# Strassen products of a SwiGLU block in another order: adding on one another in PSUM, with a growing weight sum

## The chip, the cores and the metric

The kernel runs on one core of a Trainium2 chip. The metric is the time of one execution on the device in microseconds (us). A profiled execution gives the trace that the text reads: TensorE (PE, its weight loads PEld), VectorE (DVE), ScalarE (ACT), GpSimd (POOL), SyncE (SP, which here issues the DMAs), and the DMA queues.

## The reference

One decoder layer in fp32 on 512 tokens of width 2048: an RMS norm, an input projection, three token mixers, an output projection onto the residual, and a SwiGLU feed-forward part of inner width 5632.

```python
x = x + mix @ w_out[l]
h2 = _rms_norm(x, norm2_g[l])
x = x + (jax.nn.silu(h2 @ w_gate[l]) * (h2 @ w_up[l])) @ w_down[l]
```

The change touches the last of these lines alone.

## The kernel before

Each fp32 product is made of three matmuls: every operand is split into a high part (fp32r) and a low rest, and high x high, high x low and low x high are added in PSUM.

Gate, up and down go by a scheme of Strassen's kind: a product of 2 x 2 blocks is made from seven block products instead of eight, on sums of blocks of the activations (`ops`, `acts`) and of the weights. The seven are numbered 1 to 7 after the quarter that they feed; `ORDER`, line 67, is their order in a round. The results (i, k) are collected in SBUF tiles of 128 x 512, two (a = 0 and 1) to each.

- **Up** (class `Up`, from L1288): 22 rounds, u0 to u21, two for each of 11 blocks of gate and up columns, one per half of the inner dimension. The first round of a block starts the tiles (`keep`, L1312), the second adds (`add`) or subtracts (`less`). i = 1 is gate, i = 0 is up. After the second round `gate` (silu on ACT), `weigh` (a multiplication on POOL, L1386) and `turn` make the activations of down.
- **Down** (class `Down`, from L1491): 12 rounds, d0 to d11, of four or three pairs of inner blocks (`RANGES`), into tiles `y`.

A product is two units, A and B. A unit of up is 12 matmuls of 512 columns (L1304, L1306, L1307; down's are L1569 to L1571) with one weight block of 128 x 1024, in two PSUM banks. Products alternate between two pairs of banks (`outs`). A matmul with start=True begins a bank afresh; before, that is so in products 7, 1, 5 and 2, so that 4 adds to 7, 6 to 1, and 3 to 5. After each product `done` reads the two banks into the tiles; what is read is the sum so far. Product 6 (with 1 below it) is wanted in three results, so `six` (L1332 in Up, L1586 in Down) reads each of its banks three times on DVE, or in down twice on DVE and once by an ACT copy (`copy_u`, L1594) that POOL then subtracts (L1579).

**Weights.** A block arrives by DMA from SP (`pump`, L243) in one of the raw buffers named "21a", "21b", "22a", "22b", "11", "12", "sa", "sb"; a block's names 11, 12, 21, 22 are its quarters of the weight. `plus` (L169; the instruction is L172) adds two raw blocks on POOL, 128 x 1024. `split_up_to` (from L264) makes the three tiles that PE needs: wn, a copy of the high part in PSUM (ACT, L283), wh, the same in SBUF (ACT, L284), and wl, the rest (DVE, L285, the raw block minus wn). `next_unit` (L307) calls it two units ahead (`SPLIT_AHEAD`), and there are three buffers of wh and wl each. `last` says whether a split is the last reader of its raw block and gives up its buffer.

A round's 14 units have the numbers base to base + 13, A and B by turns. Their seven blocks are, before: s, 11, 22, 11, 21, 12, 11, where four sums on POOL change what stands in them: s = 21 + 11 (written out at unit base - 4 and base - 3), 21 += 22 (base, base + 1), 11 = 21 + 11 (base + 2, + 3) and 11 += 12 (base + 7, + 8). `sums` holds them by the unit at which they are written out, and each engine executes its own instructions in the order written. The dictionary `bufs` says which raw buffer holds which block, and is turned around after each round, so that a round loads while the one before computes.

**Around u0** the input of gate and up is still being prepared. DVE makes the sums of blocks of h (L1128 to L1136), the low rests of them (L1148), and the sum of squares for the norm (L97), each with both inputs in SBUF; xr is the residual (L1098).

**The last rounds** turn finished tiles by DVE transposes (`turn_back`, L1478) into tiles z that lie in raw buffers no longer used (`BACK`), and SP writes them out (`put`, L1488). The last product, 3 of d11, is cut in three pieces; its last one is transposed on PE (`sides`, L1534), copied (L1537) and written (L1556). `later(n, f, ...)` puts a call off by n units in a queue of evictions or of extras.

Of the kernel before, what the change touches and what calls it, by code (L numbers as in the profile page):

```python
# [13 lines left out]
AF = mybir.ActivationFunctionType  # L14
ALU = mybir.AluOpType
# [50 lines left out]

ORDER = (7, 1, 4, 6, 5, 2, 3)
TH = T // 2
# [48 lines left out]
def kernel(ctx: ExitStack, tc: tile.TileContext, xT, wi, wo, wgu, wd, cst_in, outT):  # L117
# [57 lines left out]
    def up_block(pair, m, half, j):  # L175
# [3 lines left out]

    bufs = {"A": dict(zip(("21", "11", "s", "22"), ("21a", "22a", "sa", "22b"))),  # L180
            "B": dict(zip(("21", "11", "s", "22"), ("21b", "11", "12", "sb")))}

    for n in range(2 * NBLOCKS):
        base = len(works)
        keys = {c: {k: (k, f"u{n}{c}") for k in ("11", "12", "21", "22", "s")} for c in "AB"}
        for k in ("21", "11", "22", "12"):
            for i, c in enumerate("AB"):
                entries.append((bufs[c]["s" if k == "12" else k], keys[c][k],
                                up_block(n // 2 * 2, 2 - int(k[0]), int(k[1]) - 1, n % 2 * 4 + 2 * i)))
        for i, c in enumerate("AB"):  # L190
# [8 lines left out]
        bufs = {c: {"21": b["22"], "11": b["21"], "s": b["s"], "22": b["11"]} for c, b in bufs.items()}  # L199

# [5 lines left out]
    for t, (g, r) in enumerate(DOWN):  # L206
        first, end = RANGES[r]
        base = len(works)
        keys, size = {}, {}
        for c, (lo, hi) in {"A": (first, first + 2), "B": (first + 2, end)}.items():  # L210
            keys[c] = {k: (k, f"d{t}{c}") for k in ("11", "12", "21", "22", "s")}
            size[c] = 4 * P * (hi - lo)
            bufs[c]["12"] = bufs[c]["s"]
        for k in ("21A", "11A", "21B", "11B", "22A", "22B", "12A", "12B"):
# [4 lines left out]
        def add(c, out, one, other, buf=None):  # L219
            return plus(keys[c][out], keys[c][one], keys[c][other], size[c], buf)  # L220

        for i, c in enumerate("AB"):
            sums[base - 4 + i].append(add(c, "s", "21", "11", bufs[c]["s"]))
            sums[base + i].append(add(c, "21", "21", "22"))
            sums[base + 2 + i].append(add(c, "11", "21", "11"))
            sums[base + 7 + i].append(add(c, "11", "11", "12"))
        works.extend((keys[c][k], last, "moves") for k, last in (
            ("s", True), ("11", False), ("22", True), ("11", False), ("21", True), ("12", True), ("11", True)) for c in "AB")
        final_bufs = bufs
        bufs = {c: {"21": b["22"], "11": b["21"], "s": b["s"], "22": b["11"]} for c, b in bufs.items()}  # L230

# [1056 lines left out]
    class Up:  # L1288
# [4 lines left out]
        def product(self, q):  # L1293
            banks = outs[:2]
            outs[:] = outs[2:] + banks
            for c in range(2):
                sums_now()
                run(evacs)
                wh, wl = next_unit()
                for a, b in enumerate(banks):  # L1300
                    high, low = slice(a * P, (a + 1) * P), slice(TH + a * P, TH + (a + 1) * P)
                    for f in range(2):
                        x, s = ops[q, self.first + 2 * c + f], slice(f * T, (f + 1) * T)
                        nc.tensor.matmul(b, x[:, high], wh[:, s], start=c == f == 0 and q in (7, 1, 5, 2), stop=False,  # L1304
                                         skip_group_check=True)
                        nc.tensor.matmul(b, x[:, high], wl[:, s], start=False, stop=False, skip_group_check=True)  # L1306
                        nc.tensor.matmul(b, x[:, low], wh[:, s], start=False, stop=c == f == 1, skip_group_check=True)  # L1307
                yield
                run(extras)
            later(0, self.done, self.first == 0, q, banks)  # L1310

        def keep(self, i, k, a, b):  # L1312
            t = self.c[i, k, a] = slot(f"b{self.n}c{i}{k}{a}")
            if a == 0:
                nc.scalar.activation(t, b, AF.Copy, scale=1.0 if i or not self.n else self.scale(k, a))
            elif i or not self.n:
                nc.vector.tensor_copy(t, b)
            else:
                nc.vector.tensor_scalar(t, b, self.scale(k, a), None, op0=ALU.mult)
# [11 lines left out]

        def six(self, by, a, b):  # L1332
            by(0, 1, a, b)
            self.less(0, a, b)
            self.less(1, a, b)

        def done(self, first, q, banks):
            if first and q == 7:
                self.c = {}
            by = self.keep if first else self.add  # L1340
            for a, b in enumerate(banks):
                if q == 7:
                    by(1, 1, a, b)
                elif q == 1:
                    by(0, 0, a, b)
                elif q == 4:
                    by(1, 0, a, b)
                elif q == 6:
                    if a:
                        later(0, self.six, by, a, b)  # L1350
                    else:
                        self.six(by, a, b)
# [6 lines left out]
            if q in (6, 5):  # L1359
                later(1, self.gate, 6 - q, queue=extras)  # L1360
            elif q == 2:
                self.dram = tc.dram_tile([T, T], F32, name=f"bd{self.n}")
# [37 lines left out]
    y = {}  # L1400
# [46 lines left out]
    for n in range(NBLOCKS):  # L1447
        blk = Up(n)
        for blk.first in (0, 4):
# [18 lines left out]
    BACK = {(1, 0, 0): ("22", "A"), (1, 1, 1): ("22", "B"), (1, 1, 0): ("21", "A"), (1, 0, 1): ("21", "B"),  # L1468
            (0, 1, 0): ("s", "A"), (0, 1, 1): ("s", "B"), (0, 0, 0): ("22", "A"), (0, 0, 1): ("22", "B")}

# [20 lines left out]
    class Down:  # L1491
# [9 lines left out]
        def product(self, k, q):  # L1501
            banks = outs[:2]
            outs[:] = outs[2:] + banks
            fresh = q in (7, 1, 5, 2)
            tail = self.end and k == 6
# [70 lines left out]

        def add(self, i, k, a, src, eng=nc.vector, op="tensor_add"):
            t = y[self.sum(i, k, a)]
            getattr(eng, op)(t, t, src)  # L1579

        def less(self, i, k, a, src, eng=nc.vector):
            self.add(i, k, a, src, eng, "tensor_sub")

        def six(self, a, b):
            self.less(1, 1, a, b)
            self.add(0, 1, a, b)  # L1586
            if self.end:
                self.less(1, 0, a, b)
            else:
                later(0, self.copy_u, a, b, queue=extras)  # L1590

        def copy_u(self, a, b):
            u = slot(f"d{self.t}u{a}")
            nc.scalar.copy(u, b)  # L1594
            later(0, self.less, 1, 0, a, u, nc.gpsimd)

        def done(self, q, banks):
            for a, b in enumerate(banks):
                if q == 7:
                    self.add(1, 1, a, b)  # L1600
                elif q == 1:
                    self.add(0, 0, a, b)
                elif q == 4:
                    self.add(1, 0, a, b)
                elif q == 6:
                    if a:
                        later(0, self.six, a, b)
                    else:
                        self.six(a, b)
                elif q == 5:  # L1610
# [108 lines left out]
```

## Time and profile before

| | us |
|---|---|
| three runs | 1843.78, 1844.95, 1843.36 |
| their median | 1843.78 |
| span of the profiled execution | 1840.0 |
| of this, up (576.4 to 1414.3) | 837.9 |
| of this, down (1414.3 to the last matmul, 1834.5) | 420.2 |
| PE busy | 1832.2 |
| DVE, ACT, POOL busy | 1430.0, 1313.4, 1019.0 |

In the rows of the trace's timelines the first number is the start, the second the duration, both in us; then come engine, line and operation, out<-in by the program's names (buffer numbers left out), the shapes, and in brackets how long the engine was idle before and what released it. DMA issues and waits are not counted as busy. A matmul's printed duration is longer than its share of PE, since matmuls are pipelined: the distance of starts is what counts.

### The profile page before, as it was taken

The page shows a single profiled execution, that of the slowest core. Times are in us where ns is not written, and L with a number is a line of the kernel's source. Part 1 is how long each engine was busy: PE and PEld are TensorE (multiplying, and loading weights), DVE is VectorE, ACT ScalarE, POOL GpSimd, SP SyncE. Part 2 cuts the span into 40 slices and gives each one's busy share as a digit, 9 for nine tenths or more (in the row PEclk, how much of TensorE's full clock was granted, in tenths as well). Part 3 has the DMA queues.
Part 4 walks back from the last instruction along what each step waited for, and adds up shares of the span by engine and source line. Part 5 has one row for each costly group of instructions (what it writes and reads, how often), then busy time and mean ns, then how long its engine had stood idle before and what let it go on. Part 6 is the DMA issues. An engine that isn't in the chain of part 4 may idle for free.

```text
span 1840.0 us, 26561 instructions
## 1 busy us (share of the span) xinstructions
PE 1832.2 (100%) x8314; PEld 1521.0 (83%) x8314; DVE 1430.0 (78%) x2023; ACT 1313.4 (71%) x1784; POOL 1019.0 (55%) x793
## 2 busy tenths in 40 slices
PE   9999999999999999999999999999999999999998
PEld 7888888888888888888888888888888888888887
DVE  6689888986689877777777777777777777777777
ACT  6355644553468788887888888888887778877775
POOL 0126543110003557886887767787776558776552
PEclk9999999999999999999999999999999999999999
DMA  7353255363343466777867778677687579877635
GB/s 276 88 150 121 88 145 156 107 178 132 118 138 104 115 160 183 203 205 183 227 179 210 209 185 224 174 207 210 178 273 255 200 232 294 252 259 259 237 121 109
DMA packets 401612, 337.81 MB, mean 184 GB/s; under 512 B 185408, under 2 KB 327872, under 8 KB 401472
## 3 DMA queue, kind: packets, MB, share of 16 engines
q1 hardware_dynamic: 400896, 335.33, 62.9%
q8 instruction: 66, 1.08, 0.2%
q10 hardware_dynamic: 576, 0.79, 0.1%
q14 instruction: 74, 0.61, 0.1%
HBM read 261.61 MB, written 66.03 MB: 178 GB/s over the span
## 4 chain that ended last, share of the span: by engine, by line
PE 73%; DVE 1%; DMA 0%; issue 0%; ACT 0%; DVEq 0%; SPq 0%
PE out L1307 15%; PE out L1304 15%; PE out L1306 15%; PE out L1570 7%; PE out L1569 7%; PE out L1571 7%; PE o L322 2%; PE o L324 2%; PE o L323 2%; DVE y L1579 0%; DVE wl L285 0%; DMA out_T<-z 0%; DVE z L1478 0%; DVE lnv L412 0%; DVE y L1548 0%
## 5 line engine op out<-in xcount | busy, mean ns | idle before, releaser
L1304 PE MATMUL out<-wh,h 128*128 128x512 f32 x1232 | 479.2, 389 | 0.0
L1306 PE MATMUL out<-wl,h 128*128 128x512 f32 x1232 | 479.2, 389 | 0.0
L1307 PE MATMUL out<-wh,h 128*128 128x512 f32 x1232 | 479.2, 389 | 0.0
L1306 PEld LDWEIGHTS out<-wl,h 128*128 128x128 f32 x1232 | 231.2, 188 | 48.1
L1307 PEld LDWEIGHTS out<-wh,h 128*128 128x128 f32 x1232 | 231.2, 188 | 48.1
L1304 PEld LDWEIGHTS out<-wh,h 128*128 128x128 f32 x1232 | 231.2, 188 | 47.9
L1570 PE MATMUL out<-wl,a 128*128 128x512 f32 x620 | 240.4, 388 | 0.1
L1569 PE MATMUL out<-wh,a 128*128 128x512 f32 x620 | 240.4, 388 | 0.0
L1571 PE MATMUL out<-wh,a 128*128 128x512 f32 x620 | 240.3, 388 | 0.0
L289 ACT CAST wh<-w 128x1024 fp32r<-128x1024 f32 (+2 forms) x94 | 97.0, 1031 | 134.3 <-PE o L323 46.0
L1579 DVE TENSOR_TENSOR y<-y,out 128x512 f32<-128x512 f32 x192 | 128.4, 684 | 46.8 <-PE out L1571 45.0
L263 DVE TENSOR_TENSOR wl<-w,wh 128x1024 fp32r<-128x1024 f32 (+2 forms) x95 | 114.4, 1204 | 34.0 <-ACT wh L289 33.8
L1570 PEld LDWEIGHTS out<-wl,a 128*128 128x128 f32 x620 | 116.4, 188 | 24.2 <-DVE wl L285 0.5
L1569 PEld LDWEIGHTS out<-wh,a 128*128 128x128 f32 x620 | 116.4, 188 | 24.1
L1571 PEld LDWEIGHTS out<-wh,a 128*128 128x128 f32 x620 | 116.4, 188 | 23.8
L573 DVE SCALAR_TENSOR_TENSOR y<-bu,cst,y 128x511 f32<-128x511 f32 (+14 forms) x120 | 88.9, 741 | 1.1
L322 PE MATMUL o<-mh_c,wh 128*128 128x512 f32 x128 | 51.0, 398 | 0.0
L322 PE MATMUL cq<-hh,wh 128*128 128x512 f32 x128 | 50.3, 393 | 0.0
L324 PE MATMUL o<-mh_c,wl 128*128 128x512 f32 x128 | 50.0, 391 | 0.0
L323 PE MATMUL o<-ml_c,wh 128*128 128x512 f32 x128 | 50.0, 390 | 0.0
L323 PE MATMUL cq<-hl,wh 128*128 128x512 f32 x128 | 49.9, 390 | 0.0
L324 PE MATMUL cq<-hh,wl 128*128 128x512 f32 x128 | 49.9, 390 | 0.0
(2353 smaller groups left out, 4745.0 us busy)
## 6 DMA issues: line engine op xcount, KB each, us to landing
od<-a SPq DMA_DIRECT2D x154, 256.0 KB
a<-od SPq DMA_DIRECT2D x154, 256.0 KB
w<-in_wi SPq DMA_DIRECT2D x58, 512.0 KB
w<-in_wo SPq DMA_DIRECT2D x32, 512.0 KB
x<-in_xT SPq DMA_DIRECT2D x16, 256.0 KB
xr<-in_xT SPq DMA_DIRECT2D x16, 256.0 KB
x2d<-xr SPq DMA_DIRECT2D x16, 256.0 KB
z<-x2d SPq DMA_DIRECT2D x64, 64.0 KB
```

What stands on the lines that cost most here:

```text
L263: fn(*args)
L289: (nc.vector.tensor_copy if u == 0 else nc.scalar.copy)(hi[:, :n], t[:, :n])
L322: nc.tensor.matmul(out, wh, xh, start=start, stop=False)
L323: nc.tensor.matmul(out, wh, xl, start=False, stop=False)
L324: nc.tensor.matmul(out, wl, xh, start=False, stop=stop)
L1304: nc.tensor.matmul(b, x[:, high], wh[:, s], start=c == f == 0 and q in (7, 1, 5, 2), stop=False, skip_group_check=True)
L1306: nc.tensor.matmul(b, x[:, high], wl[:, s], start=False, stop=False, skip_group_check=True)
L1307: nc.tensor.matmul(b, x[:, low], wh[:, s], start=False, stop=c == f == 1, skip_group_check=True)
L1569: nc.tensor.matmul(b[:, lo:hi], x[:, high], wh[:, s], start=start, stop=False, skip_group_check=True)
L1570: nc.tensor.matmul(b[:, lo:hi], x[:, high], wl[:, s], start=False, stop=False, skip_group_check=True)
L1571: nc.tensor.matmul(b[:, lo:hi], x[:, low], wh[:, s], start=False, stop=last, skip_group_check=True)
L1579: getattr(eng, op)(t, t, src)
```

## The change

The products come in the order 1, 7, 6, 4, 5, 2, 3, and three of them begin a bank: 1, 7 and 2. On the pair of banks of 1, products 6, 5 and 3 are added; on that of 7, product 4; product 2 stands alone on the other pair. So the sum in PSUM after each product is just what one result wants, and every bank is read once for each product. `six`, `copy_u` and the POOL subtraction are gone. The tile (1, 0) of a first round begins as the negative of a bank, by a scale of -1 in `keep`.

The weight blocks are 11, s, s, 22, 21, 12, s. s = 21 + 11 is now followed by s += 22 and, at the end, s += 12 in the same buffer, and 21 += 22 in between. A round's 11 is done with after its first product; 12 comes into its buffer. The units at which the sums are written out move too.

In the last rounds the transposes and puts of the first two results take other places in the queues, and the tiles z of (0, 1) lie where 11 lay.

```diff
-ORDER = (7, 1, 4, 6, 5, 2, 3)
+ORDER = (1, 7, 6, 4, 5, 2, 3)
+FRESH = (1, 7, 2)
...
-    bufs = {"A": dict(zip(("21", "11", "s", "22"), ("21a", "22a", "sa", "22b"))),
-            "B": dict(zip(("21", "11", "s", "22"), ("21b", "11", "12", "sb")))}
+    bufs = {"A": dict(zip(("11", "21", "s", "22"), ("21b", "21a", "22a", "22b"))),
+            "B": dict(zip(("11", "21", "s", "22"), ("11", "sa", "12", "sb")))}
+
+    def use(base, size, keys, c, early):
+        i, key, buf = "AB".index(c), keys[c], bufs[c]["s"]
+        sums[base - early + i].append(plus(key["s"], key["21"], key["11"], size[c], buf))
+        sums[base + 1 + i].append(plus(key["s"], key["s"], key["22"], size[c]))
+        sums[base + 3 + i].append(plus(key["21"], key["21"], key["22"], size[c]))
+        sums[base + 7 + i].append(plus(key["s"], key["s"], key["12"], size[c]))
+
+    BLOCKS = (("11", True), ("s", False), ("s", False), ("22", True), ("21", True), ("12", True), ("s", True))
+
+    def turn_bufs():
+        return {c: {"11": b["22"], "21": b["21"], "22": b["11"], "s": b["s"]} for c, b in bufs.items()}
...
-        for i, c in enumerate("AB"):
-            key = keys[c]
-            sums[base - 4 + i].append(plus(key["s"], key["21"], key["11"], 1024, bufs[c]["s"]))
-            sums[base + i].append(plus(key["21"], key["21"], key["22"], 1024))
-            sums[base + 2 + i].append(plus(key["11"], key["21"], key["11"], 1024))
-            sums[base + 7 + i].append(plus(key["11"], key["11"], key["12"], 1024))
-        works.extend((keys[c][k], last, "moves") for k, last in (
-            ("s", True), ("11", False), ("22", True), ("11", False), ("21", True), ("12", True), ("11", True)) for c in "AB")
+        for c in "AB":
+            use(base, {"A": 1024, "B": 1024}, keys, c, 2 if n else 5)
+        works.extend((keys[c][k], last, "moves") for k, last in BLOCKS for c in "AB")
...
-    def keep(self, i, k, a, b):
+    def keep(self, i, k, a, b, sign=1.0):
...
-    def six(self, by, a, b):
-        by(0, 1, a, b)
-        self.less(0, a, b)
-        self.less(1, a, b)
...
+                if q == 1:
+                    by(0, 0, a, b)
+                elif q == 7:
                     by(1, 1, a, b)
...
+                elif q == 6:
+                    if first:
+                        self.keep(1, 0, a, b, -1.0)
+                    else:
+                        self.less(0, a, b)
                 elif q == 4:
...
+                    self.add(1, 0, a, b)
                 elif q == 5:
                     self.less(1, a, b)
+                elif q == 2:
+                    self.add(0, 0, a, b)
                 else:
-                    self.add(0, q - 2, a, b)
+                    by(0, 1, a, b)
...
-        def copy_u(self, a, b):
-            u = slot(f"d{self.t}u{a}")
-            nc.scalar.copy(u, b)
-            later(0, self.less, 1, 0, a, u, nc.gpsimd)
...
-            if self.end and q == 6:
+            if self.end and q == 4:
...
-                        later((2, 3, 6, 7)[n] + a, turn_back, self.sum(i, k, a))
-                    later((4, 5, 8, 9)[n], put, self.g, i, k, queue=extras)
+                        later((4, 5, 6, 7)[n] + a, turn_back, self.sum(i, k, a))
+                    later((6, 7, 8, 9)[n], put, self.g, i, k, queue=extras)
```

Lines of the changed kernel are two further on here (L172 is L173, L285 is L287, L1148 is L1150, L1317 is L1319; further down L1478 is L1477, L1548 is L1547, and the add and the subtraction of y are L1578 and L1582).

POOL in u0, before; w('21', 'u0A') is the raw block 21 of round u0, unit A:

```order
L172 TENSOR_TENSOR w('s', 'u0A')_5765<-w('21', 'u0A')_5556,w('11', 'u0A')_5609 128x1024
L172 TENSOR_TENSOR w('s', 'u0B')_5814<-w('21', 'u0B')_5559,w('11', 'u0B')_5664 128x1024
L172 TENSOR_TENSOR w('21', 'u0A')_5556<-w('21', 'u0A')_5556,w('22', 'u0A')_5817 128x1024
L172 TENSOR_TENSOR w('21', 'u0B')_5559<-w('21', 'u0B')_5559,w('22', 'u0B')_5872 128x1024
L172 TENSOR_TENSOR w('11', 'u0A')_5609<-w('21', 'u0A')_5556,w('11', 'u0A')_5609 128x1024
L172 TENSOR_TENSOR w('11', 'u0B')_5664<-w('21', 'u0B')_5559,w('11', 'u0B')_5664 128x1024
L172 TENSOR_TENSOR w('11', 'u0A')_5609<-w('11', 'u0A')_5609,w('12', 'u0A')_5881 128x1024
L172 TENSOR_TENSOR w('11', 'u0B')_5664<-w('11', 'u0B')_5664,w('12', 'u0B')_5933 128x1024
```

and in the changed kernel:

```order
L173 TENSOR_TENSOR w('s', 'u0A')_5710<-w('21', 'u0A')_5559,w('11', 'u0A')_5504 128x1024
L173 TENSOR_TENSOR w('s', 'u0B')_5767<-w('21', 'u0B')_5713,w('11', 'u0B')_5661 128x1024
L173 TENSOR_TENSOR w('s', 'u0A')_5710<-w('s', 'u0A')_5710,w('22', 'u0A')_5817 128x1024
L173 TENSOR_TENSOR w('s', 'u0B')_5767<-w('s', 'u0B')_5767,w('22', 'u0B')_5881 128x1024
L173 TENSOR_TENSOR w('21', 'u0A')_5559<-w('21', 'u0A')_5559,w('22', 'u0A')_5817 128x1024
L173 TENSOR_TENSOR w('21', 'u0B')_5713<-w('21', 'u0B')_5713,w('22', 'u0B')_5881 128x1024
L173 TENSOR_TENSOR w('s', 'u0A')_5710<-w('s', 'u0A')_5710,w('12', 'u0A')_5878 128x1024
L173 TENSOR_TENSOR w('s', 'u0B')_5767<-w('s', 'u0B')_5767,w('12', 'u0B')_5933 128x1024
```

The sums into 21 moved from the second place to the third. The second pair now reads and writes s, which the splits of units 2 and 3 read before; the third pair waits for no split; the last pair writes s, which the splits of units 4 and 5 read, where before it wrote 11, which those of units 6 and 7 read.

DVE in u0, before, from the end of the preparation's eight short operations to the weights of units 6 and 7:

```order
L1134 TENSOR_TENSOR ta_5950<-h_7_5924,h_15_6076 128x256
L1135 TENSOR_TENSOR tb_6128<-ta_5950,h_7_5924 128x256
L1136 TENSOR_TENSOR tb_6128<-tb_6128,h_15_6076 128x256
L1317 COPY b0c_6136<-out_5993 128x512
L285 TENSOR_TENSOR wl_6142<-w('11', 'u0A')_5609,wn_6143 128x1024
L285 TENSOR_TENSOR wl_6160<-w('11', 'u0B')_5664,wn_6161 128x1024
```

and in the changed kernel, with the weights of units 4 and 5 ahead of them:

```order
L287 TENSOR_TENSOR wl_6083<-w('s', 'u0A')_5710,wn_6084 128x1024
L287 TENSOR_TENSOR wl_6102<-w('s', 'u0B')_5767,wn_6103 128x1024
L1150 TENSOR_TENSOR h_6_6063<-ta_5901,h_6_6063 128x256
L1150 TENSOR_TENSOR h_6_6065<-tb_5977,h_6_6065 128x256
L1150 TENSOR_TENSOR h_6_6067<-h_14_5973,h_6_6067 128x256
L1150 TENSOR_TENSOR h_6_6069<-tb_5977,h_6_6069 128x256
L1150 TENSOR_TENSOR h_6_6071<-h_14_5973,h_6_6071 128x256
L1136 TENSOR_TENSOR ta_5950<-h_7_5924,h_15_6075 128x256
L1137 TENSOR_TENSOR tb_6124<-ta_5950,h_7_5924 128x256
L1138 TENSOR_TENSOR tb_6124<-tb_6124,h_15_6075 128x256
L1319 TENSOR_SCALAR b0c_6133<-out_5993 128x512
L287 TENSOR_TENSOR wl_6136<-w('22', 'u0A')_5817,wn_6137 128x1024
```

DVE's instructions stand where they stood, with other weights: units 6 and 7 now take 22, which is no sum, and units 4 and 5 take s where they took 22.

DVE in d11, around the reads of the fourth product (6 before, 4 now), before:

```order
L1579 TENSOR_TENSOR y<-y,out_5990 128x512 x3
L285 TENSOR_TENSOR wl_17767<-w('12', 'd11A')_17552,wn_17768 128x1024
L1478 STREAM_TRANSPOSE z_17761<-y 128x16x32
L1579 TENSOR_TENSOR y<-y,out_5991 128x512 x3
L1478 STREAM_TRANSPOSE z_17792<-y 128x16x32
L285 TENSOR_TENSOR wl_17795<-w('12', 'd11B')_17572,wn_17796 128x1024
L285 TENSOR_TENSOR wl_17817<-w('11', 'd11A')_17414,wn_17818 128x1024
L1478 STREAM_TRANSPOSE z_17792<-y 128x16x32
```

and in the changed kernel:

```order
L1578 TENSOR_TENSOR y<-y,out_5990 128x512
L1578 TENSOR_TENSOR y<-y,out_5991 128x512
L287 TENSOR_TENSOR wl_17590<-w('12', 'd11A')_17374,wn_17591 128x1024
L1477 STREAM_TRANSPOSE z_17585<-y 128x16x32
L1477 STREAM_TRANSPOSE z_17612<-y 128x16x32
L287 TENSOR_TENSOR wl_17615<-w('12', 'd11B')_17396,wn_17616 128x1024
L287 TENSOR_TENSOR wl_17637<-w('s', 'd11A')_17364,wn_17638 128x1024
L1477 STREAM_TRANSPOSE z_17612<-y 128x16x32
```

Ahead of the weights of 12 stand two reads of PSUM where six stood, four fewer; the transposes and weights behind them keep their order.

More of the change, by code (lines that the diff above doesn't have):

```diff
@@ L217 @@
             entries.append((bufs[c][k[:2]], keys[c][k[:2]], [down_block(g, int(k[0]) - 1, int(k[1]) - 1, *span)]))
[L219 to L228, printed above, removed]
+        for c in "AB":
+            use(base, size, keys, c, 2)
+        works.extend((keys[c][k], last, "moves") for k, last in BLOCKS for c in "AB")
         final_bufs = bufs
-        bufs = {c: {"21": b["22"], "11": b["21"], "s": b["s"], "22": b["11"]} for c, b in bufs.items()}
+        bufs = turn_bufs()
     splits = {}
@@ L1303, in product @@
                         x, s = ops[q, self.first + 2 * c + f], slice(f * T, (f + 1) * T)
-                        nc.tensor.matmul(b, x[:, high], wh[:, s], start=c == f == 0 and q in (7, 1, 5, 2), stop=False,
+                        nc.tensor.matmul(b, x[:, high], wh[:, s], start=c == f == 0 and q in FRESH, stop=False,
                                          skip_group_check=True)
@@ L1330, in less @@
             nc.vector.tensor_sub(t, t, b)
-        def six(self, by, a, b):
-            by(0, 1, a, b)
-            self.less(0, a, b)
-            self.less(1, a, b)
         def done(self, first, q, banks):
-            if first and q == 7:
+            if first and q == 1:
                 self.c = {}
@@ L1575, in sum, with add, less @@
             return self.g, i, k, a
-        def add(self, i, k, a, src, eng=nc.vector, op="tensor_add"):
+        def add(self, i, k, a, src):
             t = y[self.sum(i, k, a)]
[L1579 to L1590, printed above, removed]
-        def copy_u(self, a, b):
-            u = slot(f"d{self.t}u{a}")
-            nc.scalar.copy(u, b)
-            later(0, self.less, 1, 0, a, u, nc.gpsimd)
+            nc.vector.tensor_add(t, t, src)
+        def less(self, i, k, a, src):
+            t = y[self.sum(i, k, a)]
+            nc.vector.tensor_sub(t, t, src)
         def done(self, q, banks):
             for a, b in enumerate(banks):
-                if q == 7:
+                if q == 1:
+                    self.add(0, 0, a, b)
+                elif q == 7:
                     self.add(1, 1, a, b)
-                elif q == 1:
-                    self.add(0, 0, a, b)
+                elif q == 6:
+                    self.less(1, 0, a, b)
                 elif q == 4:
                     self.add(1, 0, a, b)
[L1605 to L1609, printed above, removed]
                 elif q == 5:
```

34 lines of the change are left out of this document (13 added, 21 removed).

## The prediction

> **What bounds the kernel now.** First I read the page's busy shares and the windows by stage (busy time and number of instructions of PE, PEld, DVE, ACT, POOL, then granted clock).
>
> ```profile
> PE 1832.2 (100%) x8314; PEld 1521.0 (83%) x8314; DVE 1430.0 (78%) x2023; ACT 1313.4 (71%) x1784; POOL 1019.0 (55%) x793
> ```
>
> ```profile
> 576.40:1414.30 837.90, 837.90 (x3699) 693.79 (x3698) 643.90 (x741) 696.33 (x844) 614.16 (x420) 1.00 0.71 195
> 1827.60:1840.00 12.40, 7.00 (x42) 5.51 (x40) 6.78 (x13) 0.70 (x3) 0.00 (x0) 0.91 0.78 153
> ```
>
> TensorE works through all of the up stage, at full clock. The stage has 22 rounds of 14 units: 837.90 / 308 = 2.72 us a unit, 0.227 for each of its 12 matmuls, 38.09 a round. The change keeps every matmul, so work saved on other engines shortens nothing there. Time can only be lost, where a unit's weights come late, or won behind 1827.6, where PE waits. The view of PE's waits has one in that stretch:
>
> ```profile
> PE sides L1534 <- DVE y L1548: 0.6, 1, 0.6
> ```
>
> So I ask of each unit whether its wl, the last step of its weights, is there in time. The least slack is where rounds begin: u0 still shares DVE with the preparation of the input. PE's timeline gives u0's start and the first matmul of unit 6 that reads wl; then DVE's and POOL's timelines of before.
>
> ```profile
> 576.52 0.39 PE L1304 MATMUL out<-wh,h 128*128 128x512 f32 x1
> 593.07 0.39 PE L1306 MATMUL out<-wl,h 128*128 128x512 f32 x1
> ```
>
> ```profile
> 580.62 2.14 DVE L97 TENSOR_TENSOR ssum<-ssum,sr 128x512 f32<-128x512 f32 x1
> ...
> 587.11 0.42 DVE L1148 TENSOR_TENSOR h<-ta,h 128x256 fp32r<-128x256 f32 x1
> 587.44 0.42 DVE L1148 TENSOR_TENSOR h<-tb,h 128x256 fp32r<-128x256 f32 x1
> 587.78 0.42 DVE L1148 TENSOR_TENSOR h<-h,h 128x256 fp32r<-128x256 f32 x1
> 588.11 0.42 DVE L1148 TENSOR_TENSOR h<-tb,h 128x256 fp32r<-128x256 f32 x1
> ...
> 590.03 0.68 DVE L1317 COPY b0c<-out 128x512 f32<-128x512 f32 x1
> 590.64 1.21 DVE L285 TENSOR_TENSOR wl<-w('11', 'u0A')_5609,wn 128x1024 fp32r<-128x1024 f32 x1
> ```
>
> ```profile
> 579.80 2.42 POOL L172 TENSOR_TENSOR w('11', 'u0A')_5609<-w('21', 'u0A')_5556,w('11', 'u0A')_5609 128x1024 f32<-128x1024 f32 x1 [7.78 <-DVE wl L285]
> 582.17 2.87 POOL L172 TENSOR_TENSOR w('11', 'u0B')_5664<-w('21', 'u0B')_5559,w('11', 'u0B')_5664 128x1024 f32<-128x1024 f32 x1
> 591.98 2.42 POOL L172 TENSOR_TENSOR w('11', 'u0A')_5609<-w('11', 'u0A')_5609,w('12', 'u0A')_5881 128x1024 f32<-128x1024 f32 x1 [6.94 <-ACT wh L284]
> ```
>
> Unit 6's wl ends at 590.64 + 1.21 = 591.85, 1.2 us ahead of 593.07. From 585.04 to 591.98 POOL did nothing, and just there DVE ran eight short operations with both inputs in SBUF (five of L1148, L1134 to L1136).
>
> **Two engines, one turn at a time.** Such operations and POOL's sums do not run together. DVE's and POOL's timelines around the first sum:
>
> ```profile
> 547.22 0.42 DVE L1148 TENSOR_TENSOR h<-ta,h 128x256 fp32r<-128x256 f32 x1
> 547.55 2.62 DVE L1148 TENSOR_TENSOR h<-h,h 128x256 fp32r<-128x256 f32 x1
> ```
>
> ```profile
> 547.43 2.46 POOL L172 TENSOR_TENSOR w('s', 'u0A')_5765<-w('21', 'u0A')_5556,w('11', 'u0A')_5609 128x1024 f32<-128x1024 f32 x1 [68.13 <-DVE wl L263]
> ```
>
> The sum came up while one L1148 ran, and the next took 2.62 us, ending 0.28 after the sum. DVE had a further operation ready and POOL still got in. The reverse stands above: L97 came up during one sum, ended at 582.76, and the sum behind it took 2.87. I read this as taking turns, whoever has waited longest. The Trainium skill (SBUF — State Buffer, Who interferes with whom) says that a DVE instruction with two SBUF inputs and a GpSimd one that reads SBUF exclude each other for a whole instruction; the rows agree, and on who comes next it says nothing.
>
> **The change part by part.**
>
> *Readout.* It drops 88 evictions of up and 26 of down on DVE. The nearest row is down's add, at 684 ns: 114 x 0.684 = 78 us of DVE's 1430.
>
> ```profile
> L1579 DVE TENSOR_TENSOR y<-y,out 128x512 f32<-128x512 f32 x192 | 128.4, 684 | 46.8 <-PE out L1571 45.0
> ```
>
> With it go 22 ACT copies and 22 POOL subtractions. All lie beside a PE that is never idle in these stages: nothing. Negating a kept product is a scale on an existing instruction, counted as nothing; if it cost 0.1 us on each of 22, DVE has more time to spare than that.
>
> *Loads.* SP issues as many, of the same sizes, for other buffers. 12 waits for 11's, given up by unit 1 of the round as s's was. The next round's 21 waits for 21's, given up by the split of unit 9, some three units ahead of unit 9's own start, and its first sum is emitted at unit 12: about 16 us for a load. Nothing, unless a load takes longer than that.
>
> *Sums and order.* Eight sums a round as before. What was 21+=22 early in the round is now s+=22 after s's first use, 21+=22 follows, and s+=12 comes last. In u0 POOL finds six sums ready in a row. The first two (s+=22) stand where the two 11 sums stood: to 585.04. Then:
>
> - 21A follows at POOL's pitch (579.80 to 582.17, 2.37): to 587.41. DVE's first short operation is at the door at about 587.3 and ends 0.28 behind the sum, 587.69.
> - 21B gets in, 2.28 us (from L97's end, 582.76, to 585.04): 589.97. The second operation: 590.25.
> - s+=12 for A: 592.53; third operation 592.81. s+=12 for B: 595.09; fourth operation 595.37.
> - POOL has nothing more. Before, from the end of the fourth operation (588.11 + 0.42) to the end of wl took 591.85 - 588.53 = 3.32: 598.7.
>
> Unit 6 then waits from 593.07 to 598.7: **5.6 us**. PE is the bound afterwards, so nothing gives this back. With two sums let in by turns the same working gives 596.5, 3.4 us; with one 1.2; with none, that is DVE's eight run through, 592.0, which is in time. Ends 0 and 5.6; I take 5.6, as the rows at 547 and 582 both show the turn changing after one operation.
>
> *The clock after that idle.* No row shows an idle of PE in mid-kernel. Ahead of its first work, PE's weight loads and matmuls, and at the end PE's last work and the window behind it, show:
>
> ```profile
> 1.12 3.59 PE L348 MATMUL idle<-idle 128*128 128x512 bf16 x8 [1.12 <-DVE nhalf L352]
> ...
> 1.95 0.15 PEld L348 LDWEIGHTS <-idle 128*128 128x128 bf16 x1 [0.28 <-issue]
> ...
> 3.65 0.15 PEld L348 LDWEIGHTS <-idle 128*128 128x128 bf16 x1 [0.28 <-issue]
> ```
>
> ```profile
> 8.35 0.39 PE L322 MATMUL in<-hh,wh 128*128 128x512 f32 x1
> 8.58 0.39 PE L323 MATMUL in<-hl,wh 128*128 128x512 f32 x1
> ```
>
> ```profile
> 1834.98 0.41 PE L1534 MATMUL sides<-ident,y 128*128 128x128 f32 x2 [0.60 <-DVE y L1548]
> ```
>
> ```profile
> 1836.00:1840.00 4.00, 0.00 (x0) 0.00 (x0) 0.00 (x0) 0.09 (x1) 0.00 (x0) 0.71 0.54 132
> ```
>
> 512 columns took (3.65 - 1.95) / 4 = 0.425 us at first and 0.23 later: about half speed after idleness. At the end the granted clock is 0.71 over 4 us; half speed for 0.58 of them means that it fell some 2.3 us after PE's last work at 1835.4. An idle of 5.6 us is longer. Slow work lasted between 3.0 us (1.12 to beyond 4.08) and 7.2 (to 8.35); I take the eight matmuls' 3.6: 3.6 x (1 - 0.227/0.425) = **1.7 us**, bounds 0 (clock kept) and 3.4. The Trainium skill (TensorE: Matmul & The Clock Gate, Part 1) states half rate after an idle window of about 3.4 us until a busy one; by that an estimate is 3.4 x 0.47 = 1.6.
>
> *Tail.* DVE is behind in d11; PE and DVE show it:
>
> ```profile
> 1829.08 0.39 PE L1569 MATMUL out<-wh,a 128*128 128x512 f32 x1
> 1829.54 0.50 PE L1570 MATMUL out<-wl,a 128*128 128x512 f32 x1
> ...
> 1832.00 0.28 PE L1570 MATMUL out<-wl,a 128*128 128x256 f32 x1
> 1832.12 0.28 PE L1571 MATMUL out<-wh,a 128*128 128x256 f32 x1
> 1832.52 0.44 PE L1534 MATMUL sides<-ident,y 128*128 128x128 f32 x2
> ```
>
> ```profile
> 1828.28 1.21 DVE L285 TENSOR_TENSOR wl<-w('11', 'd11B')_17437,wn 128x1024 fp32r<-128x1024 f32 x1
> ...
> 1830.61 1.28 DVE L1478 STREAM_TRANSPOSE z<-y 128x512 f32<-128x512 f32 x2
> 1831.82 0.65 DVE L1548 TENSOR_TENSOR y<-y,out 128x512 f32<-128x512 f32 x1
> ```
>
> The last wl lands at 1829.49 and costs PE 0.23 over its pitch (0.46 for 0.227); the late y L1548 delays sides by about 0.28 (1832.52, where the pitch of 0.12 gives 1832.24). Product 6 is read once in place of three times, up to four evictions fewer ahead of the backlog, 4 x 0.65 = 2.6 us. The wl is needed a microsecond before its present end, so both gaps close, and the transposes that feed SP's output puts are ready up to 1 us earlier. Between 0 (DVE still late, or puts that moved to later queue places crowd SP) and -1.2: I take **-0.9**.
>
> **Sum:** the profiled span, 1840.0, lies 3.8 us below the runs' median, 1843.78, an offset that I keep: 1840.0 + 5.6 + 1.7 - 0.9 = 1846.4, and 1850.2 us as a time.
>
> **The rivals.**
>
> 1. *DVE keeps its turn* (not slower). If its eight operations, issued 0.33 us apart, leave no opening for POOL, u0 has no stall and only the tail is left: 1842.9. The point is the second sum let in: with one the loss is 1.2 (1844.1, no difference that could be told), with two 3.4, or 5.1 if the clock falls (1846.3 to 1848.0). For it: eight in a row, shorter than any sum. Against: the row at 547.55.
> 2. *The idle comes, the clock stays*: 1848.5. For it: no row shows a fall in mid-kernel; against: 2.3 us sufficed at the end.
> 3. *The longer chain of s is late in every second round.* s must be split, added to, and split again. POOL and DVE of u6, before:
>
> ```profile
> 807.91 2.41 POOL L172 TENSOR_TENSOR w('21', 'u6B')_7878<-w('21', 'u6B')_7878,w('22', 'u6B')_8095 128x1024 f32<-128x1024 f32 x1
> 810.28 2.56 POOL L1386 TENSOR_TENSOR b2c<-b2c,b2c 128x512 f32<-128x512 f32 x2
> ```
>
> ```profile
> 805.87 1.21 DVE L285 TENSOR_TENSOR wl<-w('11', 'u6A')_7956,wn 128x1024 fp32r<-128x1024 f32 x1
> ```
>
> s+=22 for A must now wait for that wl (807.08), about where POOL comes free anyhow, 807.9; behind it queue two multiplications and s+=22 for B, to 807.91 + 2.41 + 2.56 + 2.41 = 815.3. A split of 1.0 on ACT and 1.2 on DVE brings its wl to about 817.5. u6 began near 576.52 + 6 x 38.09 = 805.1, unit 5 starts 13.6 later, 818.7: 1.2 us spare. If ACT or POOL ran over by 1.7, each of 11 such rounds would pay 0.5: +5.5 more, near 1855.7 with the stall.
>
> **How the numbers follow.** Forecast (three sums in, clock falls) 0.42: 1850.2, own range 1848.2 to 1852.8 (clock 0 with tail -1.2, clock 3.4 with tail 0). Clock stays 0.10; two sums in 0.08; one or none 0.32; the chain in every second round 0.06; faster through something unseen 0.02. Low end 1842.8 takes in the no-stall case, without which 3 in 10 would be left out; the high end is the likeliest case's, 1852.8. One part in 500, 3.7 us, is what a measurement of this kernel tells from no change. Slower: 0.42 + 0.10 + 0.08 + 0.06 = 0.66; same 0.32; faster 0.02.
>
> **What would show it.** Right: in u0 four of the eight L1150/L1136 operations take about 2.6 us each, POOL's sums of u0 run from 579.8 to about 595 with DVE operations between them, PE idles about 5.6 us ahead of unit 6's wl matmul, starts 0.43 apart behind it for some microseconds, and a last matmul 0.6 earlier relative to d11's start. Wrong: eight operations at 0.42 with one wait ahead of them, or a unit that waits in each even round.

## The result and the profile after

The changed kernel took 1856.69 us (median of four runs, 1855.83 to 1860.88) against 1843.57 before: a ratio of 1.0078, 95% interval 1.0063 to 1.0092. That is 13.1 us slower, where 6.4 were forecast. The direction, the clock and the tail came as worked out, and the stall in u0 came a little shorter; a loss of about the same size as u0's, which the forecast held only as its third rival, came on top.

The page's busy shares, and the view of PE's waits, of the changed kernel (new lines: L1306, L1308 and L1309 are the matmuls of up):

```profile
PE 1840.9 (99%) x8314; PEld 1522.6 (82%) x8314; DVE 1361.5 (73%) x1909; ACT 1302.9 (70%) x1762; POOL 989.7 (53%) x771
```

```profile
PE out L1308 <- DVE wl L287: 4.5, 1, 4.5
PE out L1306 <- ACT wh L286: 1.3, 6, 0.2
```

DVE is 68 us lighter and nothing came of it. In up PE now waits once for wl, for long, and in further places shortly for wh. Before, it waited there not at all.

**u0.** DVE's and then POOL's timeline of the changed kernel, as those shown of before:

```profile
588.30 1.22 DVE L287 TENSOR_TENSOR wl<-w('s', 'u0B')_5767,wn 128x1024 fp32r<-128x1024 f32 x1 [0.67 <-ACT wn L285]
589.44 1.83 DVE L1150 TENSOR_TENSOR h<-ta,h 128x256 fp32r<-128x256 f32 x1
591.19 2.63 DVE L1150 TENSOR_TENSOR h<-tb,h 128x256 fp32r<-128x256 f32 x1
593.74 2.61 DVE L1150 TENSOR_TENSOR h<-h,h 128x256 fp32r<-128x256 f32 x1
596.27 0.41 DVE L1150 TENSOR_TENSOR h<-tb,h 128x256 fp32r<-128x256 f32 x1
...
598.79 1.21 DVE L287 TENSOR_TENSOR wl<-w('22', 'u0A')_5817,wn 128x1024 fp32r<-128x1024 f32 x1
```

```profile
588.58 2.40 POOL L173 TENSOR_TENSOR w('21', 'u0B')_5713<-w('21', 'u0B')_5713,w('22', 'u0B')_5881 128x1024 f32<-128x1024 f32 x1
590.95 2.58 POOL L173 TENSOR_TENSOR w('s', 'u0A')_5710<-w('s', 'u0A')_5710,w('12', 'u0A')_5878 128x1024 f32<-128x1024 f32 x1
593.49 2.58 POOL L173 TENSOR_TENSOR w('s', 'u0B')_5767<-w('s', 'u0B')_5767,w('12', 'u0B')_5933 128x1024 f32<-128x1024 f32 x1
```

Three of the eight short operations have a sum ahead of them (the forecast had four), and the second and third sum each got in behind one of them: the turns of the forecast. The first of these sums, 21+=22 of unit B, had already begun when the first operation came, so two turns lie between the eight, not three; the wait is 4.7 us in place of 5.6. POOL's row of sums began 2.15 us into u0 (581.00, u0 begins at 578.85), where the forecast took 3.28 from before. PE's timeline there:

```profile
595.17 0.39 PE L1306 MATMUL out<-wh,h 128*128 128x512 f32 x1
600.06 0.50 PE L1308 MATMUL out<-wl,h 128*128 128x512 f32 x1 [4.50 <-DVE wl L287]
600.39 0.43 PE L1309 MATMUL out<-wh,h 128*128 128x512 f32 x1
600.62 0.63 PE L1306 MATMUL out<-wh,h 128*128 128x512 f32 x1
601.05 0.63 PE L1308 MATMUL out<-wl,h 128*128 128x512 f32 x1
...
603.61 0.59 PE L1308 MATMUL out<-wl,h 128*128 128x512 f32 x1
604.03 0.39 PE L1309 MATMUL out<-wh,h 128*128 128x512 f32 x1
```

600.06 - 595.17 less a pitch of 0.23 is 4.7 us. Behind it starts are 0.42 to 0.43 apart until 604.03: half speed, 1.7 us lost. Summing what each start is later than the pitch, u0 loses 6.4 us.

**The rounds behind.** The same sum over each round gives 1.3 for u4, 1.2 for u6, 1.1 for u8, 0.2 for u10, 0.4 for u14, 0.6 for u16, 1.5 for u18, 0.1 for u20, nothing elsewhere: 6.2 us before rounding, in units 5, 6 and 8 of rounds that begin a block. POOL in u6 of the changed kernel (u6 begins at 815.02, its unit 5 is due at 828.6):

```profile
812.14 2.42 POOL L173 TENSOR_TENSOR w('s', 'u6B')_8090<-w('21', 'u6B')_7969,w('11', 'u6B')_7910 128x1024 f32<-128x1024 f32 x1 [2.85 <-DMA z<-x2d]
814.52 2.56 POOL L1385 TENSOR_TENSOR b2c<-b2c,b2c 128x512 f32<-128x512 f32 x2
...
819.37 2.41 POOL L173 TENSOR_TENSOR w('s', 'u6A')_8067<-w('s', 'u6A')_8067,w('22', 'u6A')_7992 128x1024 f32<-128x1024 f32 x1
821.73 2.55 POOL L1385 TENSOR_TENSOR b2c<-b2c,b2c 128x512 f32<-128x512 f32 x2
824.23 2.41 POOL L173 TENSOR_TENSOR w('s', 'u6B')_8090<-w('s', 'u6B')_8090,w('22', 'u6B')_8025 128x1024 f32<-128x1024 f32 x1
```

The order is the forecast's, but the whole row stands later: s+=22 for A starts 4.35 us into the round (2.8 in the working), and for B ends 11.6 into it (10.2 there). It begins with the first line: s of B waited until a DMA landed. The row names a read of x2d that was under way then; the load that this sum needs, 21 of unit B, has its last piece at 811.98 in the trace. In u18 the row names that load itself:

```profile
1272.82 2.42 POOL L173 TENSOR_TENSOR w('s', 'u18B')_12452<-w('21', 'u18B')_12331,w('11', 'u18B')_12272 128x1024 f32<-128x1024 f32 x1 [3.46 <-DMA w('21', 'u18B')_12331<-in_wgu]
```

Before, the same sum of u6 (which begins there at 805.00) stood 7.8 us ahead of its round, where it is now 2.9:

```profile
797.22 2.42 POOL L172 TENSOR_TENSOR w('s', 'u6B')_8066<-w('21', 'u6B')_7878,w('11', 'u6B')_7990 128x1024 f32<-128x1024 f32 x1 [3.29 <-DMA w('11', 'u6B')_7990<-in_wgu]
```

How far this sum starts ahead of its round and what the round then loses go together: 4.1 us ahead and nothing lost in u12, 3.6 and 0.6 in u16, 2.9 and 1.2 in u6, 2.6 and 1.5 in u18. From u4 on, the two add up to 4.1 in every round that begins a block but u20 (3.3 and 0.1).

In u6, ACT, which takes its work in order, then splits late, and PE waits for wh:

```profile
826.68 1.02 ACT L285 CAST wn<-w('s', 'u6B')_8090 128x1024 fp32r<-128x1024 f32 x1 [2.87 <-POOL w('s', 'u6B')_8090 L173]
827.63 1.05 ACT L286 CAST wh<-w('s', 'u6B')_8090 128x1024 fp32r<-128x1024 f32 x1
```

wh of unit 5 lands at 828.68, after its due time; ACT does not catch up, and unit 8 starts at 837.73, 0.6 behind the matmul ahead of it and 0.37 over its pitch. What held the first sum is in SP's queue; the split of 21 of u5's unit B on DVE is what gives up the buffer:

```profile
796.23 1.22 DVE L287 TENSOR_TENSOR wl<-w('21', 'u5B')_7613,wn 128x1024 fp32r<-128x1024 f32 x1 [0.92 <-PE out L1309]
```

```profile
797.76 0.92 SPq L245 DMA_DIRECT2D w('21', 'u6A')_7936<-in_wgu  x2
798.72 4.05 SPq L1255 DMA_DIRECT2D p3r<-bd  x4
802.87 1.41 SPq L1239 DMA_DIRECT2D od<-a  x2
804.38 0.96 SPq L245 DMA_DIRECT2D w('21', 'u6B')_7969<-in_wgu  x2
...
806.49 6.23 SPq L1418 DMA_DIRECT2D z<-x2d  x4
```

The buffer was free at 797.45. The load was issued at 804.38, behind four reads of the pair's activations and two writes, and beside four reads of x2d it took until 812.0: the first sum of s could not start earlier.

**The tail.** DVE's last split and the last y that PE waits for, and PE around sides:

```profile
1842.16 1.21 DVE L287 TENSOR_TENSOR wl<-w('s', 'd11B')_17388,wn 128x1024 fp32r<-128x1024 f32 x1
...
1845.70 0.68 DVE L1547 TENSOR_TENSOR y<-y,out 128x512 f32<-128x512 f32 x1
```

```profile
1846.81 0.28 PE L1570 MATMUL out<-wh,a 128*128 128x256 f32 x1
1846.93 0.38 PE L1533 MATMUL sides<-ident,y 128*128 128x128 f32 x2
```

Sides follows at the pitch of 0.12; before, there were 0.40. (The wait of 0.6 that the prediction quotes from the view of waits belongs to the second half of sides, and it is still there.) From the first matmul of down (1429.33, before 1414.28) the split stands 1.17 us earlier. To the span's end there are 424.8 us, before 425.7: 0.9 won, as forecast.

The two profiled executions differ by 14.1 us: 6.4 in u0, 6.2 in the rounds behind, -0.9 in the tail, and 2.3 ahead of u0, of which 2.2 arise in the first 12 us, where the code is the same; that part is told at the end.

### The profile page after: what moved, and what is told of

It is laid out like the page before. It is cut to its first block, busy times and chain, and to the rows that moved or that the text cites. A ratio compares the mean times of both kernels' runs of the same rounds, so it can differ in the third digit from the quotient of the medians.

```text
span 1854.1 us, 26421 instructions
## 1 busy us (share of the span) xinstructions
PE 1840.9 (99%) x8314; PEld 1522.6 (82%) x8314; DVE 1361.5 (73%) x1909; ACT 1302.9 (70%) x1762; POOL 989.7 (53%) x771
## 4 chain that ended last, share of the span: by engine, by line
PE 62%; POOL 5%; DMA 3%; ACT 1%; issue 1%; SPq 1%; DVE 1%; POOLq 0%; ACTq 0%; DVEq 0%
PE out L1306 11%; PE out L1308 11%; PE out L1309 11%; PE out L1570 8%; PE out L1568 8%; PE out L1569 8%; PE o L326 2%; PE o L324 2%; PE o L325 2%; POOL a L1232 1%; DMA z<-x2d 1%; ACT wn L285 1%; ACT wh L286 0%; DVE h L1150 0%; SPq L1255 0%
## 5 line engine op out<-in xcount | busy, mean ns | idle before, releaser
L1308 PE MATMUL out<-wl,h 128*128 128x512 f32 x1232 | 481.4, 391 | 4.5 <-DVE wl L287 4.5
L1306 PE MATMUL out<-wh,h 128*128 128x512 f32 x1232 | 481.6, 391 | 1.3 <-ACT wh L286 1.3
L1309 PE MATMUL out<-wh,h 128*128 128x512 f32 x1232 | 480.0, 390 | 0.0
L1306 PEld LDWEIGHTS out<-wh,h 128*128 128x128 f32 x1232 | 231.5, 188 | 54.9 <-ACT wh L286 7.0
L1308 PEld LDWEIGHTS out<-wl,h 128*128 128x128 f32 x1232 | 231.7, 188 | 54.4 <-DVE wl L287 5.2
L1309 PEld LDWEIGHTS out<-wh,h 128*128 128x128 f32 x1232 | 231.7, 188 | 47.7
L1578 DVE TENSOR_TENSOR y<-y,out 128x512 f32<-128x512 f32 x118 | 80.2, 686 | 36.4 <-PE out L1570 35.2
```

## The experiments

Theory A: in u0 the turns between DVE and POOL cause the 6.4. Theory B: in the rounds that begin a block, s+=22 is late; B1 says by late loads of 21, B2 by POOL's queue as such.

**Sums held back in u0.** A small copy on POOL reads the end of DVE's eight operations, ahead of three sums.

```diff
+    def wait_for_h():
+        t = cp.tile([P, 1], F32, name="seen")
+        nc.gpsimd.tensor_copy(t, mark[0][:, :1])
...
+        if n == 0:
+            sums[base + 4].append(wait_for_h)
...
         nc.vector.tensor_add(n4, n2, h21)
+        mark[:] = [n4]
```

> In u0 POOL gets a small copy (128x1) that reads the result of the last of DVE's eight short operations, ahead of the 21+=22 sum of unit B: that sum and the two s+=12 sums can start only when the eight are done. Theory A (POOL and DVE take turns at the door, one operation each, and three sums got in between the eight): no operation of the eight waits behind those sums, unit 6's wl is in time, the 6.4 us that PE lost at unit 6 of u0 (4.7 of waiting, 1.7 at half clock) go to under 0.5, and the time falls from 1856.7 to about 1850.3. Rival A2 (unit 6 is late because its round's chain of s is late, whatever the eight do): PE still waits 3 us or more at unit 6, time above 1853.5. Both leave the 6.1 us of the later rounds as they are.

1851.09 us, ratio to before 1.0047 (1.0031 to 1.0064): 5.6 us less than the changed kernel. DVE and POOL there:

```profile
588.78 0.42 DVE L1160 TENSOR_TENSOR h<-ta,h 128x256 fp32r<-128x256 f32 x1
589.11 0.42 DVE L1160 TENSOR_TENSOR h<-tb,h 128x256 fp32r<-128x256 f32 x1
...
592.31 1.21 DVE L295 TENSOR_TENSOR wl<-w('22', 'u0A')_5817,wn 128x1024 fp32r<-128x1024 f32 x1
```

```profile
591.86 0.18 POOL L200 COPY seen<-tb 128x1 f32<-128x1 f32 x1 [3.91 <-DVE tb L1147]
592.00 2.42 POOL L173 TENSOR_TENSOR w('21', 'u0B')_5713<-w('21', 'u0B')_5713,w('22', 'u0B')_5881 128x1024 f32<-128x1024 f32 x1
```

The eight run 0.33 to 0.46 us apart, wl lands in time, and u0 loses nothing. A holds, A2 falls: the chain in u0 was as it had been. The later rounds lose 8.5 us in this execution (6.2 in the changed kernel's); the size of that loss differs from profile to profile.

**Two sums earlier in u0.** 21+=22 goes ahead of s+=22 in u0.

```diff
-        sums[base + 3 + i].append(plus(key["21"], key["21"], key["22"], size[c]))
+        sums[base + (3 + i if early == 2 else 0)].append(plus(key["21"], key["21"], key["22"], size[c]))
```

> In u0 alone the two sums 21+=22 are written out ahead of s+=22, where POOL was idle; so only the two s+=12 sums are left that can meet DVE's eight short operations. Theory A: the first of the eight waits for the first s+=12, one sum gets in behind it, the rest run free; the wait of PE at unit 6 falls from 4.7 to about 1.6 us, too short for the clock to fall, so u0 loses 1.6 in place of 6.4: about 1851.9. Rival A3 (the two engines do not alternate, POOL simply comes first whenever it has sums): both sums go ahead of all eight, unit 6 waits about as long as for one more sum, 4 us, time above 1854. Rival A2: unchanged, 1856.7.

1855.73 us (one run), which as a time is near the rivals' figures and not near the 1851.9 of theory A. The trace says why. DVE:

```profile
590.61 0.44 DVE L1150 TENSOR_TENSOR h<-ta,h 128x256 fp32r<-128x256 f32 x1
590.97 2.63 DVE L1150 TENSOR_TENSOR h<-tb,h 128x256 fp32r<-128x256 f32 x1
593.52 0.41 DVE L1150 TENSOR_TENSOR h<-h,h 128x256 fp32r<-128x256 f32 x1
```

One sum got in, behind the first operation, and the rest ran free: turns, not POOL first (A3 falls). But u0 lost 4.0 us and not 1.6. PE idled 2.3, because wl of unit 5, just ahead of the eight, ended at 590.69, 1.2 later than in the changed kernel (589.52): its sum on POOL had started later, at 585.51 and not 583.37. And the clock fell all the same (starts 0.43 apart), which the expectation had excluded. The later rounds lost 8.6 here, which is the rest of why the time stayed high.

**Loads a unit earlier.**

```diff
         split_up_to(u + SPLIT_AHEAD)
+        if ahead:
+            pump(RAW_BUFS, 2)
```

> SP may issue up to two raw loads also right behind a unit's split, so that a load whose buffer that split gives up is issued one unit earlier. Theory B1 (the second rounds of a pair, u4, u6, u8 and so on, are late because 21 of unit B lands late, POOL's first sum of s waits for it, and everything behind it on POOL moves back 1.5 us): the 6.1 us lost in these rounds fall below 2, time about 1852. Rival B2 (POOL's own queue between the uses of s is too long even with the blocks in time): they stay at 5 to 6, time 1855.5 to 1857. u0's 6.4 stays in both.

1848.60 us, ratio 1.0029 (1.0018 to 1.0040): 8.1 us less than the changed kernel, more than the 6.2 of its one profile and about what the two other profiles lost there. No round behind u0 loses anything; u0 still loses 6.4. SP and POOL in u6, which there begins at 811.15:

```profile
796.46 0.91 SPq L245 DMA_DIRECT2D w('21', 'u6B')_7945<-in_wgu  x2
797.42 3.60 SPq L1257 DMA_DIRECT2D p3r<-bd  x4
```

```profile
805.10 2.41 POOL L173 TENSOR_TENSOR w('s', 'u6B')_8093<-w('21', 'u6B')_7945,w('11', 'u6B')_7886 128x1024 f32<-128x1024 f32 x1
...
813.37 2.42 POOL L173 TENSOR_TENSOR w('s', 'u6A')_8067<-w('s', 'u6A')_8067,w('22', 'u6A')_7978 128x1024 f32<-128x1024 f32 x1 [1.01 <-ACT wn L285]
815.73 2.57 POOL L1387 TENSOR_TENSOR b2c<-b2c,b2c 128x512 f32<-128x512 f32 x2
818.25 2.41 POOL L173 TENSOR_TENSOR w('s', 'u6B')_8093<-w('s', 'u6B')_8093,w('22', 'u6B')_8001 128x1024 f32<-128x1024 f32 x1
```

The load now stands ahead of the four reads, s of B starts 6.05 us ahead of the round and not 2.9, and s+=22 for B ends 9.5 us into it. POOL then even waits for ACT, and the order of work on POOL is as it was, with the multiplications ahead of s+=22 for B. B1 holds.

**Less ahead of the sum on POOL.**

```diff
-                later(0, self.weigh, q - 2)
-                later(2, self.turn, q - 2)
-                later(3, self.store, q - 2, queue=extras)
+                late = 2 * (q == 3)
+                later(late, self.weigh, q - 2)
+                later(2 + late, self.turn, q - 2)
+                later(3 + late, self.store, q - 2, queue=extras)
...
-                ...(5, 13, 0))
+                ...(7, 13, 0))
```

> The second pair of multiplications of a block (weigh for product 3), with the transposes, the store and the reads behind it, is put off by two units, so that it and the three half-tile sums of the pair stand behind s+=22 of unit B on POOL and no longer ahead of it. Theory B2 (POOL's own queue is what makes s+=22 late): s+=22 for B ends some 2.5 us earlier, the 6.1 us lost in u4, u6, u8, u18 and the others fall below 1, time about 1851. Theory B1 (late loads alone): the first sum of s is as late as before and the loss falls only in part, 2 to 4 us left, time about 1853 to 1855. u0's 6.4 stays in both.

1848.91 us, ratio 1.0031 (1.0020 to 1.0043); no round behind u0 loses. So B2's number came too: s+=22 for B ends 7.0 us into u6 (818.07 + 2.41, begun at 813.45). But the edit did not leave the loads as they were. It puts the four reads of the pair's activations off as well, and these had stood ahead of the load of 21 in SP's queue. SP and POOL in u6:

```profile
798.44 2.21 SPq L245 DMA_DIRECT2D w('21', 'u6B')_7956<-in_wgu  x2
...
805.73 5.17 SPq L1255 DMA_DIRECT2D p3r<-bd  x4
```

```profile
808.19 2.42 POOL L173 TENSOR_TENSOR w('s', 'u6B')_8089<-w('21', 'u6B')_7956,w('11', 'u6B')_7896 128x1024 f32<-128x1024 f32 x1
```

The load is issued 15.0 us ahead of the round (10.6 in the changed kernel, 14.7 with the loads a unit earlier), and the first sum of s starts 5.3 ahead of it. The expectation's "as late as before" for that sum did not hold, so this run cures by B1's way too and says nothing for B2. That the late load took the margin rests on the run before it; whether a shorter queue on POOL alone would be enough was not tried.

**Both cures:** the copy in u0 and the earlier loads.

> Both cures together: the small POOL copy that holds u0's sums back until DVE's eight short operations are done, and raw loads issued one unit earlier. If the two causes are all that the change lost, no round of up waits any longer and only the shorter tail is left: 1843.4 - 0.9 = 1842.5, a ratio of 0.9995. If something else of the change costs time that these two covered (a next late split at unit 8, or the tail), 1844 or more.

1841.44 us against 1842.55, ratio 0.9993 (0.9984 to 1.0003). No unit of up waits, and nothing else of the change is seen to cost time. What is left, 1.1 us less than before, is about the tail's size, and the interval does not exclude that it is nothing.

**The order alone**, with the weight sums and buffers of before. The cut shows the blocks against the kernel before; the order of products and the readout are those of the change.

```diff
-            ("s", True), ("11", False), ("22", True), ("11", False), ("21", True), ("12", True), ("11", True)) for c in "AB")
+            ("11", False), ("s", True), ("11", False), ("22", True), ("21", True), ("12", True), ("11", True)) for c in "AB")
```

> The order of the products and the single readout alone: the weight sums, their units and the raw buffers are those of before (s = 21+11 used once, 11 = 21+11 after 21 += 22, then 11 += 12), only the blocks stand in the new order. Theory: the later rounds lose nothing, since 21 has its buffer early and the first sum of s comes four units ahead; in u0 the two sums 11 += 12 are now ready when DVE's eight come, one of them gets in behind the first operation: a wait of 1.2 to 2.1 us at unit 6, and 0 to 1.9 by the clock; time 1843.6 to 1846.4. Rival (the order itself is at fault, for instance as 22's buffer, which the next 21 takes, comes free a product later): the later rounds lose 2 us or more together, time above 1846.5.

1945.40 us, ratio 1.0553 (1.0539 to 1.0568). The theory fails here by far, and the rival's sign is right but not its reason. Nearly all is lost at unit 4: 8 to 10 us in each round that begins a block from u4 to u18, and up to 3 in the rounds between. In u0, 6.5 are lost where 1.2 to 4.0 were expected: one sum got in between the eight, as expected, but the eight began only 13.6 us into u0 (10.6 in the changed kernel), behind late splits of units 4 and 5. SP, POOL and ACT in u6, which begins there at 827.05:

```profile
824.39 1.16 SPq L244 DMA_DIRECT2D w('22', 'u6A')_8044<-in_wgu  x2
```

```profile
830.64 2.41 POOL L173 TENSOR_TENSOR w('21', 'u6A')_7877<-w('21', 'u6A')_7877,w('22', 'u6A')_8044 128x1024 f32<-128x1024 f32 x1 [1.36 <-DMA w('22', 'u6B')_8071<-in_wgu]
...
840.14 2.34 POOL L173 TENSOR_TENSOR w('11', 'u6A')_7936<-w('21', 'u6A')_7877,w('11', 'u6A')_7936 128x1024 f32<-128x1024 f32 x1
```

```profile
842.51 1.02 ACT L284 CAST wn<-w('11', 'u6A')_7936 128x1024 fp32r<-128x1024 f32 x1 [10.24 <-POOL w('11', 'u6A')_7936 L173]
```

Product 6 is now third and needs 11 + 21 + 22 two units earlier. With the sums of before it stands behind both sums 21+=22, and these behind the load of 22, whose buffer is the last to come free; in the rounds that begin a block, multiplications and half-tile sums of the block before stand between them too. The new sum, s+=22, needs one sum behind that load, and 22 gets the buffer of 12, free a product earlier. So the order needs the growing s, or something else that has product 6's weights ready in time; the run changes sums and buffers together and does not say how much each of them does.

**The order alone, sums held back in u0.**

> The order alone, as in the run beside it, with the small POOL copy in u0 ahead of the two sums 11 += 12. Theory: nothing waits in up, the tail stays 0.9 shorter: 1842.5. If the later rounds lose in the order alone, that loss shows here by itself, 1844.5 or more.

1937.88 us, ratio 1.0518 (1.0504 to 1.0532). The loss of the later rounds stands by itself, and u0's falls from 6.5 to 2.5: waits of about 1 us at units 2 and 6, where none was expected. With this order the copy does not free u0 altogether.

## Why the prediction fell short

- **What bounds the kernel, and the readout:** right. 78 us of work off DVE, 68 measured, bought nothing in up.
- **Turns in u0:** right in mechanism, taken away by one POOL copy. The size: 4.7 for 5.6, since POOL's row of sums began 1.1 us earlier in the round than the forecast took it, and one of the three sums was already under way.
- **The clock:** 1.7 forecast and measured. That half speed follows the idle was right; that the size fitted to a tenth was luck in part, since other long idles in these runs were followed by losses of 1.4 to 2.8.
- **The tail:** -0.9 forecast and measured, with the split a microsecond earlier and the first gap at sides closed, as the steps said.
- **Loads: this step failed.** It said "about 16 us for a load. Nothing, unless a load takes longer than that". The 16 us were counted from the place of unit 9's split to that of the sum in the program. The split's end on DVE, at 797.45, and the issue, at 804.38, lie 7 us apart, because the load is written out only after the next unit's start and SP takes its work in order; landing took 7.6 more. 14.7 us had gone by when the sum started, 2.9 us ahead of the round. To cost nothing it had to start 4.1 ahead, as u12 shows, which is 13.5 us after the split's end: that was the room, not 16.
- **Rival 3** followed from it. Its chance, 0.06, was far too low. Its price, 1855.7, is near the measured 1856.7 by luck in good part: it took 0.5 us in each of 11 rounds for an overrun of ACT or POOL by 1.7, and the rounds lost between 0 and 1.5, by a late load. The working of the chain gave 1.2 us of spare time on the condition that POOL stands where it stood before; with loads in time (9.5 us into u6 and no loss) that was borne out. The condition was not.
- **The range** ended at 1852.8, as if the chain and the stall could not come together.

The offset of 3.8 us between the first profile and the median was no fixed offset either: the listed runs are 1.7 us over their spans, and the other 2.1 are about the size of a start that runs slowly in some executions and not in the first profile.

## What to carry to other kernels

A rotation of buffers is priced at the queue that refills them: when the buffer is free, behind what the load stands in its in-order queue, and when it lands, each read from rows, not from the place in the program. A margin of about 1 us in a chain through three in-order engines is no margin if a transfer feeds it, and its chance should say so. And sums that become ready in a row on GpSimd are dangerous where VectorE runs a train of short operations with two inputs in SBUF: here one sum got in after each of them, at 2.2 us a time, until POOL had no more.

## What the runs showed of the hardware

- **Short idles and the clock.** Counting the starts of PE over all kernels here, every idle of 3.8 us and more in up was followed by 7 to 13 matmuls at 0.43 us, 1.4 to 2.8 us lost. Of six idles of 2.0 to 2.7 us only one was, the 2.3 us of the second experiment; none of 1.3 us and less. The Trainium skill (TensorE: Matmul & The Clock Gate, Part 1) speaks of an idle window of about 3.4 us that runs freely; a shorter idle that still lowered the clock differs from that.
- **Turns.** The Trainium skill (SBUF — State Buffer, Who interferes with whom) says that the port pair that VectorE and GpSimd share is an exclusive lock, and that the order of issue decides who blocks. The runs agree, 2.6 us for a 0.42 us operation, and add that with both queues full one instruction of each went in turn.
- **The start.** In some executions the first matmuls of real work run at half speed for longer: four of L518 took 2.08 us in the changed kernel's profile, the same four of L516 1.21 in the first, and everything behind them stands 2.3 us later. Of the nine profiles of this case, six have the slow start. The repeated runs of the kernel before lie near 1841.6 and 1843.4, which fits; no two profiles of one kernel are here to show it. A comparison of two single executions can be off by as much.
